# First two modulation vectors split between TensorE and VectorE, squares summed by TensorE, last value rows in groups of 256

## The chip, the cores and the metric

The kernel runs on one core of a Trainium2 chip. The metric is device time in microseconds (us), the median of several executions. One further execution is recorded by the hardware profiler; all rows below come from it. Engines: PE is TensorE (PEld its weight loads, which overlap its matmuls), DVE is VectorE, ACT is ScalarE, POOL is GpSimd, SP is SyncE, which here issues the loads of all weights. "L690" is line 690 of the kernel's file. The changed file has other line numbers.

## The reference, cut to what matters

Two layers over x of 256 rows and 2048 columns, all in fp32: the first mixes by RWKV-7, the second by banded attention, each with an MLP. Each layer takes six modulation vectors from c. The change touches the start of the first layer: the first two vectors (`sh1`, `sc1`), the norm, and the value product `xv @ w_v`.

```python
mod = c @ w_ada[layer] + b_ada[layer]
sh1, sc1, gt1, sh2, sc2, gt2 = jnp.split(mod, 6, axis=-1)
h = modulate(rms_norm(x, g_mix[layer]), sh1, sc1)     # h * (1 + scale) + shift

# rwkv7_time_mix
xx = token_shift(h) - h
xr, xw, xk, xv, xa, xg = [h + xx * mu[j] for j in range(6)]
r = xr @ w_r
k = xk @ w_k
v = xv @ w_v
w_log = -jax.nn.softplus(-(w0 + jnp.tanh(xw @ w1) @ w2)) - 0.5
a = jax.nn.sigmoid(a0 + (xa @ a1) @ a2)
g = jax.nn.sigmoid(xg @ g1) @ g2
...
```

## The kernel before

Activations lie transposed: the 2048 columns of x are 16 tiles n of 128 partitions, and the 256 rows of the sequence lie along the free dimension. Every weight comes from HBM once, in tiles of 512 KB (128 partitions by 1024 values). fp32 products are made of three passes: `halves` splits a weight tile `raw` into a rounded part wH (a cast on ACT, L378) and the rest wL (a subtraction on DVE, L381), `split` does the same for an activation (aHL), and PE adds wH by high, wH by low and wL by high. Products that PE does in plain fp32 stand as two records each in the profile.

The change lies in `layer_a`, in what runs before the key and receptance products, whose first matmul is L412 (tile pj). That stretch is a loop over the 16 tiles n. For each n it needs the modulation of these 128 columns, then it normalises and modulates h (L770 on DVE, L772 on ACT), takes the shift difference xx on POOL (L727), mixes it six times on DVE (L732 and L796), and PE multiplies: the first layers of the three small products (tile l, L779 and L783, plain fp32), and row block n of w_v for the first 1024 value columns (tile v, L787 to L789, weight rows `w_v_rows`), which adds up in PSUM over all n. The other 1024 value columns don't fit in PSUM. `v_part` does them for four n at once: each of its 16 tiles of w_v (4 groups of n by 4 blocks of 256 columns) gives one 512-wide sum in tile t (L751 to L753), which ACT copies (group 0) or DVE adds (L759) to the values in SBUF. From n = 4 on one `v_part` runs in each step; four are left at the end.

The first two modulation vectors are computed inside this loop, by `ada_blocks`, a generator that `next(adab)` drives a few tiles ahead of their use. A block is 256 columns of both vectors (`blocks` = eight times 2 column tiles). For each vector SP loads four tiles rawa (L673), each of 512 rows by 256 columns in pieces of 1 KB. Three of them go to PE: `crep` holds each value of c repeated over 32 columns, and four groups of 32 partitions of the PE array work on four row blocks at once (L690, tile m). The fourth goes to DVE, which multiplies by c and adds (L679 once, L682 three times, tile acca), and PE sums that over partitions (L684). ACT copies the block's result out (L697), PE turns it into columns and sums the four groups (L702), and DVE adds the bias and makes the gain (L708, L710). The tiles rawa have 6 buffers: the load of a tile waits until the tile six before it has been read.

The sum of squares of the norm: ACT squares (L514, L517), DVE adds (L518), PE sums over partitions with ones (L523), and `rstd` makes the reciprocal root.

The order of instructions on an engine isn't that of the code: the framework's scheduler interleaves it. SP's loads go out in its order, one behind the other; a load without a free buffer holds up all behind it. L368 is the load of all other weight tiles (raw), L763 that of the small products' weights. Later in the kernel the other ten vectors are computed on DVE alone (L452 and L454, tile acc, which has one buffer).

Of the kernel before, what the change touches and what calls it, by code (L numbers as in the profile page):

```python
# [18 lines left out]
P = 128  # L19
D = 2048  # L20
# [309 lines left out]
class Body:  # L330
# [242 lines left out]
    def run(self):  # L573
# [12 lines left out]
        for layer in (0, 1, "kv"):  # L586
            for part in range(2 if layer == "kv" else 6):
                self.mods[(layer, part)] = gp.tile([P, KT], F32, name=f"mod_{layer}_{part}")
        self.nhalf, self.pool_every = 0, 0
# [40 lines left out]
    def layer_a(self, st, sp):  # L630
# [6 lines left out]
        with ExitStack() as s1:  # L637
# [7 lines left out]
            first = CST_AT["ident"][0]  # L645
# [7 lines left out]
            crep = pb.tile([P, KT, 32], F32, name="crep")  # L653
            nc.vector.tensor_copy(crep, self.ct.unsqueeze(2).to_broadcast([P, KT, 32]))
            nc.vector.memset(h[:, :, 0:1], 0.0)
            gain = self.gp.tile([P, KT], F32, name="gain_g_mix0")

            blocks = [1] * 0 + [2] * ((KT - 0) // 2)

            def ada_blocks():  # L660
# [3 lines left out]
                for w_ in blocks:  # L664
                    W, ks = w_ * P, 8 // w_
                    ps = self.psm().rearrange("p (i n) -> p i n", i=2)
                    for part in (1, 0):
                        w, _ = self.ada_src(0, part)
                        w = w[:, lo * P:lo * P + W].rearrange("(a i p) n -> a p i n", p=P, i=ks)
                        for a in range(KT // ks):  # L670
                            raw = pb.tile([P, HK * P], F32, tag="rawa", bufs=6, name="rawa")
                            raw = raw.rearrange("p (i n) -> p i n", i=ks)
                            nc.sync.dma_start(out=raw, in_=w[a])  # L673
                            if a == KT // ks - 1:
                                acc = pb.tile([P, W], F32, tag="acca", bufs=2, name="acca")
                                for i in range(ks):
                                    ck = self.ct[:, ks * a + i:ks * a + i + 1]
                                    if i == 0:
                                        nc.vector.tensor_scalar(out=acc, in0=raw[:, i, :], scalar1=ck, scalar2=0.0,  # L679
                                                                op0=ALU.mult, op1=ALU.add)  # L680
                                    else:
                                        nc.vector.scalar_tensor_tensor(out=acc, in0=raw[:, i, :], scalar=ck, in1=acc,  # L682
                                                                       op0=ALU.mult, op1=ALU.add)
                                nc.tensor.matmul(ps[0:32, part, :W], self.cst("ones")[:, 0:32], acc,  # L684
                                                 start=False, stop=(part == 0), tile_position=(0, 0))
                            else:
                                for i in range(ks):
                                    kt = ks * a + i
                                    g = 32 * (kt % 4)
                                    nc.tensor.matmul(ps[g:g + 32, part, :W], crep[:, kt, :], raw[:, i, :],  # L690
                                                     start=(part == 1 and kt < 4),
                                                     stop=(part == 0 and g > 0 and kt >= KT - ks - 4),
                                                     tile_position=(0, g))
                            if part or a < KT // ks - 1:
                                yield
# [511 lines left out]
```

## Time and profile before

| | |
|---|---|
| median of 3 runs | 2673.8 us (2673.53 to 2674.96) |
| the profiled execution, its own time | 2673.81 us |
| its span | 2672.0 us |
| first L690, last L690 | 9.96 us, 172.37 us |
| first normalised row (L770) | 32.63 us |
| first L412 (pj) | 209.0 us |
| HBM read, mean over the span | 656.72 MB, 247 GB/s |

How to read the rows that follow. A row of windows has the stretch in us, its length, then for each engine its busy time and instructions, the TensorE clock that was granted (1.00 is full), the mean busy share of the 16 DMA engines (an estimate, which can come out a little over 1) and their rate. A row of the timeline has start, duration (of a row of several: from the first's start to the last's end), engine, line, operation, tile written and tiles read, count, and in brackets the engine's idle time ahead of it with what ended it. A row of groups has the count, then busy us and mean ns of one, then idle time. A matmul's duration contains its way through the array: matmuls in a row start every 0.12 us while each shows 0.28.

### The profile page before, as it was taken

How to read it: one execution, taken by the hardware profiler on the slowest of the kernel's cores; microseconds unless marked ns; L12 is line 12 of the kernel's file. 1: busy time of each engine (PE TensorE's matmuls, PEld its weight loads, DVE VectorE, ACT ScalarE, POOL GpSimd, SP SyncE). 2: the span in 40 equal slices, each digit the busy share in tenths (PEclk: the TensorE clock that was granted, in tenths of full speed). 3: DMA queues.
4: the chain of work that ended last, by engine and by line, in shares of the span. 5: the costliest groups of instructions: out<-in, count | busy, mean ns of one | idle time of the engine just before them, and what ended most of it. 6: DMA issues, size and time to landing. Idle time of an engine off the chain costs nothing. (4 is left out here: it accounts for less than half of the span.)

```text
span 2672.0 us, 58365 instructions
## 1 busy us (share of the span) xinstructions
PE 2600.1 (97%) x23690; PEld 2225.4 (83%) x23690; DVE 2101.0 (79%) x3109; ACT 1343.9 (50%) x2432; POOL 209.7 (8%) x320
## 2 busy tenths in 40 slices
PE   6999999999999999999999999999999999999997
PEld 3777788788899888888888998877898888888886
DVE  5778888889789888888888898899887556555555
ACT  3345555555456445355365554565564463453554
POOL 0001322332110000000000100000100000000002
PEclk9999999999999999999999999999999999999999
DMA  9966556565768888899898679887766555555553
GB/s 337 314 236 211 192 173 210 189 206 195 245 240 304 324 309 321 322 324 331 320 328 294 238 240 325 324 274 259 264 216 237 186 187 188 189 186 185 189 189 119
DMA packets 217390, 662.64 MB, mean 248 GB/s; under 512 B 21408, under 2 KB 68896, under 8 KB 217120
## 3 DMA queue, kind: packets, MB, share of 16 engines
q1 hardware_dynamic: 215056, 656.36, 71.1%
q8 instruction: 186, 3.05, 0.5%
q10 hardware_dynamic: 2064, 2.54, 0.3%
q14 instruction: 84, 0.69, 0.1%
HBM read 656.72 MB, written 2.10 MB: 247 GB/s over the span
## 5 line engine op out<-in xcount | busy, mean ns | idle before, releaser
L381 DVE TENSOR_TENSOR wL<-raw,wH 128x1024 fp32r<-128x1024 f32 x772 | 940.9, 1220 | 342.6 <-ACT wH L378 337.8
L378 ACT CAST wH<-raw 128x1024 fp32r<-128x1024 f32 x772 | 805.5, 1045 | 801.2 <-PE pj L412 646.0
L412 PE MATMUL pj<-aHL,wH 128*128 128x512 f32 x3328 | 1201.9, 403 | 2.0 <-DVE x L927 1.1
L413 PE MATMUL pj<-aHL,wL 128*128 128x256 f32 x3328 | 936.3, 281 | 0.0
L412 PEld LDWEIGHTS pj<-aHL,wH 128*128 128x128 f32 x3328 | 629.5, 189 | 154.1 <-issue 9.2
L412 PE MATMUL pj<-hHL,wH 128*128 128x512 f32 x2048 | 724.6, 399 | 0.0
L413 PEld LDWEIGHTS pj<-aHL,wL 128*128 128x128 f32 x3328 | 629.7, 189 | 2.6 <-issue 0.8
L413 PE MATMUL pj<-hHL,wL 128*128 128x256 f32 x2048 | 574.7, 281 | 0.0
L412 PEld LDWEIGHTS pj<-hHL,wH 128*128 128x128 f32 x2048 | 384.8, 188 | 95.7 <-DVE hHL L973 0.2
L413 PEld LDWEIGHTS pj<-hHL,wL 128*128 128x128 f32 x2048 | 387.0, 189 | 0.1
L454 DVE SCALAR_TENSOR_TENSOR acc<-rada,ct,acc 128x1024 f32<-128x1024 f32 x256 | 327.5, 1279 | 8.4 <-DMA rada<-w_ada 7.5
L518 POOL TENSOR_TENSOR ss<-ss,sq 128x256 f32<-128x256 f32 x56 | 54.5, 974 | 1590.8 <-ACT sq L517 1590.5
L998 DVE SCALAR_TENSOR_TENSOR x<-pj,mod,x 128x256 f32<-128x256 f32 x256 | 123.3, 482 | 59.5 <-PE pj L413 55.7
L454 DVE SCALAR_TENSOR_TENSOR acc<-raw,ct,acc 128x1024 f32<-128x1024 f32 x104 | 136.4, 1312 | 15.5 <-DMA raw<-w_ada 15.4
L401 PE MATMUL pj<-aHL,wH 128*128 128x258 f32 x384 | 109.0, 284 | 0.0
L402 PE MATMUL pj<-aHL,wH 128*128 128x258 f32 x384 | 109.0, 284 | 0.0
L970 ACT ACTIVATE t<-t 128x256 f32<-128x256 f32 x112 | 46.8, 418 | 122.6 <-DVE t L942 122.6
L403 PE MATMUL pj<-aHL,wL 128*128 128x258 f32 x384 | 108.0, 281 | 0.0
L403 PEld LDWEIGHTS pj<-aHL,wL 128*128 128x128 f32 x384 | 73.2, 191 | 0.2
L402 PEld LDWEIGHTS pj<-aHL,wH 128*128 128x128 f32 x384 | 72.6, 189 | 0.1
L401 PEld LDWEIGHTS pj<-aHL,wH 128*128 128x128 f32 x384 | 72.2, 188 | 0.2
L972 ACT ACTIVATE t<-t 128x256 f32<-128x256 f32 x128 | 53.4, 417 | 3.4
(244 smaller groups left out, 2812.3 us busy)
## 6 DMA issues: line engine op xcount, KB each, us to landing
raw<-w_up SPq DMA_DIRECT2D x256, 512.0 KB, 4.1
raw<-w_down SPq DMA_DIRECT2D x256, 512.0 KB, 4.1
rada<-w_ada SPq DMA_DIRECT2D x209, 512.0 KB, 5.7
raw<-w_ada SPq DMA_DIRECT2D x111, 512.0 KB, 4.4
rawa<-w_ada SPq DMA_DIRECT2D x64, 512.0 KB, 6.8
rada<-w_ada_kv SPq DMA_DIRECT2D x64, 512.0 KB, 6.6
raw<-w_k SPq DMA_DIRECT2D x32, 512.0 KB, 4.2
raw<-w_r SPq DMA_DIRECT2D x32, 512.0 KB, 4.5
```

What stands on the lines that cost most here:

```text
L378: nc.scalar.copy(Hf, raw)
L381: eng.tensor_tensor(out=Lf, in0=raw, in1=Hf, op=ALU.subtract)
L401: nc.tensor.matmul(ps, H[:, i, :], a(kt)[:, 0, :], start=(first and kt == 0), stop=False)
L402: nc.tensor.matmul(ps, H[:, i, :], a(kt)[:, 1, :], start=False, stop=False)
L403: ins = nc.tensor.matmul(ps, L[:, i, :], a(kt)[:, 0, :], start=False, stop=(last and kt == KT - 1))
L412: nc.tensor.matmul(ps, H[:, i, :], a(kt), start=(kt == 0), stop=False)
L413: ins = nc.tensor.matmul(ps[:, 0, :], L[:, i, :], a(kt)[:, 0, :], start=False, stop=(kt == KT - 1))
L454: nc.vector.scalar_tensor_tensor(out=self.acc, in0=raw, scalar=ck, in1=self.acc, op0=ALU.mult, op1=ALU.add)
L518: (eng or nc.gpsimd).tensor_tensor(out=self.ss, in0=self.ss, in1=sq, op=ALU.add)
L970: nc.scalar.activation(t, t, AF.Relu)
L972: nc.scalar.activation(t, t, AF.Square)
L998: nc.vector.scalar_tensor_tensor(out=x, in0=ps[:, i, :], scalar=self.mods[(layer, 5)][:, n:n + 1], in1=x, op0=ALU.mult, op1=ALU.add)
```

## The change

1. The vectors. For the first 1024 rows of w_ada, blocks of columns still go to PE (L690 in the new file too). For the other 1024 rows the host passes the weights transposed (`w_ada0_t`): a tile is 128 output columns on the partitions by 1024 rows along the free dimension, rows of 4 KB. DVE multiplies it by `crow`, those 1024 values of c on every partition, and sums along the free dimension in the same instruction (L696, `accum_out`). The result is already a column per output; DVE adds it to bias and PE's part (L711, L713). The L684 products are gone. `crow` is made at the start: DVE puts the values of c on diagonals of a 128 by 1024 tile (L665, in a buffer of rawa), PE sums it over partitions with ones (L670), ACT copies (L671). It lies in the buffer that L452 uses later.
2. The blocks are seven of 2 column tiles and two of 1. A block of 1 loads pieces of 512 bytes for PE.
3. The squares are summed by 16 matmuls with ones into one PSUM tile (L726), and the root is taken before the first block. The ones and the identity are in the first load of constants.
4. The value tiles of the last four n are cut into 2 n by 512 columns (`parts`): such a tile leaves two sums, in the PSUM tiles t and m. Four `v_part` go with the steps n = 14 and 15 (two each), two are left behind the loop.

```diff
-    def rstd(self):
+    def rstd(self, ps=None):
         nc = self.nc
-        ps = self.psm()[:, :T]
-        nc.tensor.matmul(ps, self.cst("ones"), self.ss, start=True, stop=True)
+        if ps is None:
+            ps = self.psm()[:, :T]
+            nc.tensor.matmul(ps, self.cst("ones"), self.ss, start=True, stop=True)
...
-            crep = pb.tile([P, KT, 32], F32, name="crep")
-            nc.vector.tensor_copy(crep, self.ct.unsqueeze(2).to_broadcast([P, KT, 32]))
+            crep = pb.tile([P, HK, 32], F32, name="crep")
+            nc.vector.tensor_copy(crep, self.ct[:, :HK].unsqueeze(2).to_broadcast([P, HK, 32]))
...
-            blocks = [1] * 0 + [2] * ((KT - 0) // 2)
+            sums = pb.tile([P, 2, KT], F32, name="sums01")
+            rawa = lambda: pb.tile([P, HK * P], F32, tag="rawa", bufs=6, name="rawa")
+
+            crow, diag = self.wp.tile([P, HK * P], F32, tag="acc", bufs=1, name="crow"), rawa()
+            nc.vector.tensor_tensor(out=diag.rearrange("p (k n) -> p k n", n=P),
+                                    in0=self.cst("ident").unsqueeze(1).to_broadcast([P, HK, P]),
+                                    in1=self.ct[:, HK:].unsqueeze(2).to_broadcast([P, HK, P]), op=ALU.mult)
+            for i in range(0, HK * P, 512):
+                ps = pp.tile([P, 512], F32, tag="t", bufs=1, name="t")
+                nc.tensor.matmul(ps, self.cst("ones"), diag[:, i:i + 512], start=True, stop=True)
+                nc.scalar.copy(crow[:, i:i + 512], ps)
+
+            blocks = [2] * 7 + [1] * 2
...
-                        for a in range(KT // ks):
-                            raw = pb.tile([P, HK * P], F32, tag="rawa", bufs=6, name="rawa")
-                            raw = raw.rearrange("p (i n) -> p i n", i=ks)
+                        for a in range(w_):
+                            raw = rawa().rearrange("p (i n) -> p i n", i=ks)
                             nc.sync.dma_start(out=raw, in_=w[a])
...
+                            raw = rawa()
+                            nc.sync.dma_start(out=raw, in_=d["w_ada0_t"][KT * part + lo + a])
+                            nc.vector.scalar_tensor_tensor(out=raw, in0=raw, scalar=1.0, in1=crow, op0=ALU.mult,
+                                                           op1=ALU.mult, accum_out=sums[:, part, lo + a:lo + a + 1])
...
-            self.ss_reset()
+            ss = pp.tile([P, 2, T], F32, tag="v3", bufs=1, name="v3")[:, 0, :]
             for n in range(KT):
-                self.ss_add(h[:, n, 1:T + 1], n, nc.vector)
+                sq = pb.tile([P, T], F32, tag="sq", bufs=3, name="sq")
+                nc.scalar.activation(sq, h[:, n, 1:T + 1], AF.Square)
+                nc.tensor.matmul(ss, self.cst("ones"), sq, start=(n == 0), stop=(n == KT - 1))
+            r = self.rstd(ss)
...
+            parts = [(4 * g, 4, i) for g in range(3) for i in range(4)]
+            parts[11:] = [(12, 2, 0), parts[11], (12, 2, 1), (14, 2, 0), (14, 2, 1)]
...
-                if n >= 4:
-                    v_part(n // 4 - 1, n % 4)
+                for _ in range((n >= 4) + (n >= KT - 2)):
+                    v_part()
...
-            for i in range(4):
-                v_part(3, i, "tm"[i % 2])
+            for _ in range(2):
+                v_part()
```

What the scheduler makes of it, at three places. SP's first loads (h is x, lw1 the small products' weights), before:

```order
L648 DMA h_100<-x 128x4x256 x2
L673 DMA rawa_161<-w_ada 128x4x256
L673 DMA rawa_167<-w_ada 128x4x256
L673 DMA rawa_173<-w_ada 128x4x256
L673 DMA rawa_179<-w_ada 128x4x256
L673 DMA rawa_187<-w_ada 128x4x256
```

and now:

```order
L652 DMA h_99<-x 128x4x256 x2
L781 DMA lw1_247<-lora1 128x448
L368 DMA raw_249<-w_v_rows 128x1024
L686 DMA rawa_181<-w_ada0 128x4x256
L695 DMA rawa_187<-w_ada0_t 128x1024
L686 DMA rawa_190<-w_ada0 128x4x256
L695 DMA rawa_196<-w_ada0_t 128x1024
L686 DMA rawa_199<-w_ada0 128x4x256
L695 DMA rawa_205<-w_ada0_t 128x1024
L686 DMA rawa_208<-w_ada0 128x4x256
L695 DMA rawa_214<-w_ada0_t 128x1024
L686 DMA rawa_252<-w_ada0 128x4x256
```

The small products' weights and the first value rows (which stood behind the eighth tile) have moved ahead of the first; tiles for PE and for DVE alternate. With the diagonal in the first buffer, rawa_208 takes the buffer of rawa_181.

PE at the start, before (ss is the sum of squares):

```order
L690 MATMUL m<-rawa,crep 32x256 x12
L684 MATMUL m<-acca,csts 32x256
L690 MATMUL m<-rawa,crep 32x256 x12
L684 MATMUL m<-acca,csts 32x256
L702 MATMUL m<-csts,adat 32x1 x16
L523 MATMUL m<-ss,csts 128x256
```

and now (v_122 is the sum of squares, t the copy of c):

```order
L670 MATMUL t<-rawa,csts 128x512
L726 MATMUL v_122<-sq,csts 128x256
L670 MATMUL t<-rawa,csts 128x512
L726 MATMUL v_122<-sq,csts 128x256 x3
L690 MATMUL m<-rawa,crep 32x256
L726 MATMUL v_122<-sq,csts 128x256 x12
L690 MATMUL m<-rawa,crep 32x256 x15
L706 MATMUL m<-csts,adat 32x1 x16
```

All but one of the L690 of the first block stand behind the sixteen L726 now, where the one product with ones stood behind the whole block.

PE around the last tile of the modulation, before:

```order
L690 MATMUL m_1630<-rawa_1756,crep_109 32x256 x4
L789 MATMUL v1_249<-aHL_246,wL_1801 128x256
L789 MATMUL v2_250<-aHL_246,wL_1801 128x256
L787 MATMUL v2_250<-aHL_246,wH_1800 128x256
L788 MATMUL v2_250<-aHL_246,wH_1800 128x256
L789 MATMUL v2_250<-aHL_246,wL_1801 128x256
```

and now:

```order
L690 MATMUL m_1568<-rawa_1669,crep_108 32x128 x8
L807 MATMUL v1_242<-aHL_239,wL_1705 128x256
L807 MATMUL v2_243<-aHL_239,wL_1705 128x256
L805 MATMUL v2_243<-aHL_239,wH_1704 128x256
L806 MATMUL v2_243<-aHL_239,wH_1704 128x256
L807 MATMUL v2_243<-aHL_239,wL_1705 128x256
L807 MATMUL v3_244<-aHL_239,wL_1705 128x256
L706 MATMUL m_1684<-csts_65,adat_1682 32x1 x8
```

Both stand in the middle of the products of n = 13. From that L690 to the first pj there are 234 rows before and 222 now. The last L706 follows seven rows behind its L690, where the last L702 stood 34 rows behind; the last L684, between them, is gone. From the first pj on, the order on PE is the same row for row, and so are SP's loads from the first of w_k on.

More of the change, by code (lines that the diff above doesn't have):

```diff
@@ L664, in ada_blocks @@
                 for w_ in blocks:
[L665 removed]
+                    W, ks = w_ * P, HK // w_
                     ps = self.psm().rearrange("p (i n) -> p i n", i=2)
                     for part in (1, 0):
[L668 to L694 removed]
```

78 lines of the change are left out of this document (52 added, 26 removed).

## The prediction

> **What bounds the kernel now.** The page comes first, for the whole; the question is which stretch can give or lose time.
>
> ```profile
> span 2672.0 us, 58365 instructions
> PE 2600.1 (97%) x23690; PEld 2225.4 (83%) x23690; DVE 2101.0 (79%) x3109; ACT 1343.9 (50%) x2432; POOL 209.7 (8%) x320
> ```
>
> PE is busy for 97% of the span, so time comes only from PE's own work or from stretches where it waits. The change lies ahead of the key and receptance products, whose first matmul (L412) starts at 209.0 us. The windows of that stretch, cut where its loop over n repeats (two values of n are one block of modulation columns):
>
> ```profile
> core 0: us, PE busy (x) PEld busy (x) DVE busy (x) ACT busy (x) POOL busy (x), PEclk, DMA share, GB/s
> 2.00:64.00 62.00, 38.81 (x338) 23.76 (x339) 39.72 (x91) 18.35 (x38) 2.55 (x4) 0.92 1.04 348
> 64.00:86.00 22.00, 20.91 (x194) 15.58 (x193) 15.46 (x33) 7.38 (x12) 1.90 (x2) 1.00 0.96 324
> 86.00:108.00 22.00, 21.54 (x198) 16.12 (x198) 15.54 (x33) 7.88 (x13) 1.85 (x2) 1.00 0.92 312
> 108.00:130.00 22.00, 21.62 (x200) 16.29 (x199) 16.15 (x34) 7.38 (x12) 1.85 (x2) 1.00 0.92 306
> 130.00:152.00 22.00, 20.54 (x192) 15.48 (x191) 16.41 (x35) 7.10 (x11) 1.53 (x2) 1.00 0.92 308
> 152.00:174.00 22.00, 20.98 (x195) 15.83 (x194) 16.43 (x35) 7.11 (x11) 1.54 (x2) 1.00 0.92 314
> 174.00:208.00 34.00, 32.18 (x269) 29.52 (x267) 22.04 (x36) 19.07 (x26) 1.53 (x2) 1.00 0.41 139
> ```
>
> Three parts. Up to 64 us the transfers run at 348 GB/s with nothing to spare, and PE is busy for only 38.81 of 62 us. From 64 to 174 us there are five equal cycles of 22 us: PE 21.1 us busy on average (96%), the transfers at 0.92 to 0.96, 6.9 MB a cycle. From 174 us PE works off what is left, with the transfers at 0.41. Who holds the transfers back in the middle part is in the waits of SP's queue:
>
> ```profile
> SPq L673 <- PE m L690: 54.0, 22, 4.9
> ```
>
> Tile loads wait for a buffer that PE's L690 has yet to read, 54.0 us in 110. Part of that is the ordinary wait of a queue that runs ahead, but the share falls from 1.04 to 0.92 just where PE's busy share rises to 96%, so I read the cycles as set by PE, with the transfers close behind.
>
> **The change, cycle by cycle (64 to 174 us).** What the first two vectors cost in the first and last cycle: first all that reads the raw tiles, then the L684 alone:
>
> ```profile
> 64.00:86.00 22.00, 4.23 (x48) 1.16 (x48) 3.53 (x8) 1.00 0.96 324
> 152.00:174.00 22.00, 4.23 (x48) 1.16 (x48) 3.60 (x8) 1.00 0.92 314
> 64.00:86.00 22.00, 1.24 (x4) 0.28 (x4) 1.00 0.96 324
> ```
>
> *PE.* Six tiles a cycle cost 4.23 us (0.705 each), the two sums over partitions 1.24. Now four tiles are left and L684 is gone: 2 x 0.705 + 1.24 = 2.65 us less, 21.1 becomes 18.5.
>
> *VectorE.* It spent 3.56 us a cycle on two tiles and now takes four, each in one instruction that multiplies 1024 columns and sums them. No row has that sum; the nearest is L454, of the same operation, shape and type without it:
>
> ```profile
> L454 DVE SCALAR_TENSOR_TENSOR acc<-rada,ct,acc 128x1024 f32<-128x1024 f32 x256 | 327.5, 1279 | 8.4 <-DMA rada<-w_ada 7.5
> L682 DVE SCALAR_TENSOR_TENSOR acca<-rawa,ct,acca 128x256 f32<-128x256 f32 x30 | 14.4, 479 | 0.5
> 400.00:500.00 100.00, 98.78 (x2037) 80.97 (x2032) 88.06 (x163) 54.29 (x154) 28.45 (x39) 1.00 0.64 211
> ```
>
> From below 1.28 us; from above a second pass over the columns: (1279 - 479) / 768 = 1.04 ns a column, so 1.07 us more, 2.35. I take 1.28, as L454 already reads two fp32 tensors. Four make 5.1: VectorE goes from 16.0 to 17.6 us a cycle. The two or three tiny instructions on 2 to 4 columns stay about as they were.
>
> The Trainium skill, Vector Engine (DVE) Microarchitecture Reference, section 7 (Points that are easy to get wrong), speaks against this: a scalar-tensor-tensor with two SBUF sources that are not bf16 halves its throughput, with no port left for the accumulator. L454 at 1.25 ns a column shows no halving for two sources alone; with an accumulator nothing here shows it. By the rule the instruction would cost the upper end, which is the second rival.
>
> *Transfers.* The bytes are the same, 64 tiles of 512 KB, but half come as rows of 4 KB in place of 1 KB. The price of a packet from two stretches of the DMA view, 2 to 64 us and 1100 to 1500 us (packets, MB, share of the 16 engines' time):
>
> ```profile
> q1 hardware_dynamic: 17058, 19.67, 95.0%
> q1 hardware_dynamic: 34257, 124.73, 86.7%
> ```
>
> 62 x 16 x 0.95 / 17058 = 55 ns for 1153 bytes, 400 x 16 x 0.867 / 34257 = 162 ns for 3641: 0.043 ns a byte and 6 ns a packet. A tile takes 1.59 us in 1 KB rows, 1.45 in 4 KB, 1.77 in 512-byte rows. A transposed tile saves 0.14 us, 0.55 a cycle; the four 512-byte tiles of the last two blocks, now one column tile wide, cost 0.7 together. A cycle's 6.9 MB at the 350 GB/s that the first part holds are 19.7 us, less 0.55: 19.15.
>
> So PE 18.5, VectorE 17.6, transfers 19.15: the transfers set the cycle. At the 96% that PE reaches now that is 20.0 us. Five cycles gain 2.0 each, less 0.7: **-9.3 us**. Bounds: -14 (five times 19.15, no loss) and 0 (the three disturb each other as much as now).
>
> **The start.** The squares are now added by 16 fp32 matmuls of 256 columns, ahead of most L690 in PE's order, with two of 512 columns that copy c along the partitions. SP loads the first value rows ahead of the first tile, and one of the six buffers first holds the diagonal.
>
> ```profile
> 9.96 1.08 PE L690 MATMUL m<-rawa,crep 128*32 128x256 f32 x8 [9.96 <-DMA rawa<-w_ada]
> 10.41 0.42 ACT L514 ACTIVATE ss<-h 128x256 f32<-128x256 f32 x1 [8.39 <-DMA h<-x]
> 32.63 0.88 DVE L770 SCALAR_TENSOR_TENSOR h<-h,gain_g_mix,rstd 128x256 f32<-128x256 f32 x2
> 39.58 1.56 PE L783 MATMUL l<-mix,lw 128*128 128x256 f32 x4
> 41.20 0.28 PE L787 MATMUL v<-aHL,wH 128*128 128x256 f32 x1
> 41.32 0.28 PE L788 MATMUL v<-aHL,wH 128*128 128x256 f32 x1
> 145.50 1.02 PE L779 MATMUL l<-mix,lw 128*96 128x256 f32 x4
> 146.36 1.03 PE L783 MATMUL l<-mix,lw 128*128 128x256 f32 x4
> 1.00:21.00 20.00, 3.48 (x28) 0.84 (x32) 5.81 (x15) 5.80 (x13) 0.00 (x0) 1.00 1.01 327
> ```
>
> Such a matmul (two records) takes 0.78 us early (L783 at 39.58) and 0.43 once PE runs steadily (145.50 to 146.36). Sixteen, and four more for the two wide ones, are 8.6 to 15.6 us from the first square at 10.8: done at 19.4 to 26.4. I take 22.5: PE begins without a pause, but from idle. Until then the fourth tile for PE has no buffer, and SP stands at it with all behind: the second block's tiles, the next value rows. What is issued before are about 6.8 MB (x, constants, value rows, lora, six tiles), which at 327 GB/s last until 22 us. With some 2.5 us from the release to the data, the transfers pause for 3 us (bounds 0 and 7). Against that 14 transposed tiles before 64 us save 2.0: **+1.0 us**. The first normalised row may come earlier than 32.63 us; behind transfers that are full this is worth nothing, and its cover, if it goes, is worth up to 3 us of gain. The removed 16 adds on VectorE hid behind the loads.
>
> **The tail.** From the last tile's matmuls at 172.37 us to 209.0 PE does 36.6 us.
>
> ```profile
> 172.37 0.64 PE L690 MATMUL m<-rawa,crep 128*32 128x256 f32 x8
> ...
> 174.36 0.28 PE L753 MATMUL t<-aHL,wL 128*128 128x256 f32 x1
> 174.48 0.28 PE L751 MATMUL t<-aHL,wH 128*128 128x256 f32 x1
> ...
> 175.91 0.28 PE L751 MATMUL t<-aHL,wH 128*128 128x256 f32 x1
> 176.11 0.62 PE L684 MATMUL m<-acca,csts 128*32 128x256 f32 x2
> 176.66 0.38 PE L752 MATMUL t<-aHL,wH 128*128 128x256 f32 x1
> L412 PE MATMUL pj<-aHL,wH x93: 388/397/697, 209.0 to 259.6; 128*128 128x512 f32 x93
> ```
>
> The order has 234 rows there before and 222 now: 12 x 0.12 = 1.4 us less; L684 (0.75 against 0.12) saves 0.6. The last value products leave two 512-column sums each, four adds more; VectorE has room (22.04 of 34 us), and PE fills the other bank meanwhile, so I cost them at nothing; without that cover about 0.7 us each. **-2.0 us**, bounds -2.3 and +0.8. The number of products is the same; that they come in an earlier order is what makes the 12 rows.
>
> **The sum.** -9.3 + 1.0 - 2.0 = -10.3 us. From the first pj on PE's order is the same, and PE is the bound (98.78 of 100 us in the row above), so the shift is carried whole. The profiled execution took 2673.81 us, 1.8 more than its span, and the median shown is 2673.8: 2663.5 us.
>
> **The rivals.**
>
> *The buffers keep the cycle (2669).* PE was not what held the transfers: tiles come in turns from two engines, SP issues in order, and a tile that waits in VectorE's queue behind weight halves stops everything behind it. For it: the 0.92 in cycles where PE still pauses for about 1 us. Against it: L690 as the named releaser. The cycle falls only to 21.2, five times -0.8, with start and tail -5.
>
> *VectorE becomes the bound (2686).* The accumulating instruction takes 2.35 us: 16.0 - 3.56 + 9.4 = 21.8 us a cycle. VectorE never did more than 88 of 100 us beside PE (the row of 400 to 500 us), so the cycle is 24.8, +2.8 five times, with start and tail +13. It decides from about 1.74 us an instruction on: (22 x 0.88 - 12.4) / 4. Against it: L454.
>
> *The start stalls (2672).* PE stays slow through all the sums, the transfers pause 7 us and the cycles gain only 1 each: +5 - 5 - 2.
>
> *More than the sum (2657).* The early first row lets PE run ahead, and the cycles reach 19.15.
>
> **How the numbers follow.** Chances: forecast 0.53, buffers 0.2, VectorE 0.1, start 0.07, more 0.1. 0.2% is 5.3 us, what a measurement here can tell from nothing. Faster by that, below 2668.5: nearly all of the forecast, the last rival and four tenths of the buffers: 0.70. Within: 0.21. Slower: 0.09. The range runs from the last rival's 2656 to 2675, where a mild case of VectorE ends.
>
> **What will show it.** Right: L696 at 1.3 us; cycles of about 20 us with the transfers at 0.95 or more; the last L690 near 163 us and the first pj matmul near 199. Wrong: L696 above 1.7 us; a gap in the transfers of over 5 us near 22 us; cycles still at 22 us; or the time lost again behind the first pj matmul.

## The result and the profile after

| | before | after |
|---|---|---|
| median | 2674.1 us (2670.4 to 2678.0, 20 runs) | 2669.1 us (2664.5 to 2675.5, 20 runs) |
| ratio, 95% interval | | 0.9983 (0.9977 to 0.9989) |
| span of the profiled execution | 2672.0 us | 2667.0 us |
| last L690, first pj (L412) | 172.4, 209.0 us | 169.3, 203.1 us |

The change gains 5.0 us, half of the 10.3 forecast. It is faster by 0.17% (the interval lies below 1), inside the range, and it lands on the price of a rival (2669).

The windows of the changed kernel, cut at the same times as those of the kernel before:

```profile
2.00:64.00 62.00, 45.99 (x358) 31.47 (x358) 39.87 (x82) 20.89 (x44) 4.30 (x5) 0.92 1.01 358
64.00:86.00 22.00, 19.96 (x170) 15.31 (x171) 16.70 (x34) 6.58 (x11) 1.64 (x2) 0.92 0.87 304
86.00:108.00 22.00, 19.59 (x180) 15.64 (x179) 17.45 (x34) 7.96 (x13) 1.19 (x2) 1.00 0.89 311
108.00:130.00 22.00, 19.79 (x181) 15.85 (x179) 17.41 (x34) 8.78 (x14) 1.80 (x3) 1.00 0.95 322
130.00:152.00 22.00, 19.25 (x176) 15.60 (x176) 18.59 (x37) 7.06 (x12) 1.53 (x2) 1.00 0.94 308
152.00:174.00 22.00, 20.69 (x213) 17.54 (x214) 20.33 (x45) 7.26 (x14) 2.70 (x2) 1.00 0.84 294
```

In the four windows from 64 to 152 us PE's busy time fell from 21.1 to between 19.3 and 20.0 us, and VectorE's rose from about 16 to between 16.7 and 18.6. But the transfers do not run faster: 304 to 322 GB/s, as before (306 to 324). So PE was relieved and the cycles did not follow. The groups that read rawa in the changed kernel (count, ns min/median/max, first and last start):

```profile
L690 PE MATMUL m<-rawa,crep x288: 272/379/637, 17.8 to 169.3; 128*32 128x256 f32 x112, 128*32 128x128 f32 x32
L696 DVE SCALAR_TENSOR_TENSOR rawa<-rawa,crow x32: 1209/1218/1428, 17.5 to 171.1; 128x1024 f32<-128x1024 f32 x32
L696 DVE DVE_READ_ACCUMULATOR rawa<-rawa,crow x32: 72/82/85, 18.7 to 172.2; 128x1 f32 x32
```

To see where the 5.9 us at the first pj come from, a mark for each cycle is needed. SP issues one lw load for each n; the 6th, 8th, 10th, 12th and 14th stand one block apart:

| kernel | 6th lw | 8th | 10th | 12th | 14th | mean cycle | last L690 | first pj |
|---|---|---|---|---|---|---|---|---|
| before | 63.8 | 85.5 | 107.5 | 129.5 | 152.2 | 22.1 | 172.4 | 209.0 |
| after | 61.9 | 84.4 | 106.2 | 127.4 | 149.0 | 21.8 | 169.3 | 203.1 |

The start gains 1.9 us (63.8 to 61.9), the four cycles 1.3 together, the stretch with the last block nothing, and the tail, from the last L690 to the first pj, 2.7 (36.6 to 33.9). Behind the first pj 0.9 are lost again: the spans differ by 5.0.

These marks are of one execution each. How far they can be trusted is shown by pairs of kernels of the section on the experiments that have the same order of instructions on every engine up to 150 us: the changed kernel and e3, and e2 and e5. Their marks differ by up to 1.9 us, and the four cycles together take 87.1 us in the changed kernel and 88.6 in e3 (88.4 before). So the 1.3 us of the cycles is not clear of chance. That the 14th lw comes 3 us earlier or more is: 152.2 before (154.0 in e4), 147.7 to 149.2 in the changed kernel, e1, e2, e3 and e5.

What a cycle looks like from SP and PE, in the timeline of the changed kernel (rows of other engines left out):

```profile
52.34 0.38 SPq L686 DMA_DIRECT2D rawa<-w_ada  x1
...
61.68 0.43 PE L706 MATMUL m<-csts,adat 128*32 128x1 f32 x32
...
62.87 0.50 SPq L695 DMA_DIRECT2D rawa<-w_ada_t  x1
...
64.65 0.39 PE L769 MATMUL t<-aHL,wL 128*128 128x256 f32 x1 [1.60 <-DVE wL L381]
...
66.37 2.02 PE L797 MATMUL l<-mix,lw 128*96 128x256 f32 x4 [0.63 <-DVE mix L739]
68.33 1.08 PE L690 MATMUL m<-rawa,crep 128*32 128x256 f32 x8
69.47 0.38 SPq L686 DMA_DIRECT2D rawa<-w_ada  x1
```

SP issues nothing from 62.87 to 69.47 us. It waits for the buffer of the tile that it issued at 52.34 (six loads back). That load landed after 8.5 us, so the tile lay in its buffer from 60.8 on; PE read it at 68.33, because in PE's order its L690 stand behind value products (L767 to L769) and the row's L797, and those wait for VectorE.

A second stop, 76.43 to 81.94, ends with a tile of VectorE's. The tile was issued at 62.87 and landed after 8.1 us, at 71.0, but in VectorE's order its L696 stands behind two subtractions of weight halves (L381), and these wait for value rows that SP could only issue at 71.88, after the first stop:

```profile
71.88 0.53 SPq L368 DMA_DIRECT2D raw<-w_v_rows  x1
...
78.40 2.36 DVE L381 TENSOR_TENSOR wL<-raw,wH 128x1024 fp32r<-128x1024 f32 x2 [3.19 <-DMA raw<-w_v_rows]
80.68 1.22 DVE L696 SCALAR_TENSOR_TENSOR rawa<-rawa,crow 128x1024 f32<-128x1024 f32 x1
81.94 0.33 SPq L695 DMA_DIRECT2D rawa<-w_ada_t  x1
```

So the stops feed each other: a late reader holds up the queue, the loads behind it go out late, and the engines that wait for those are the next late readers. The profile's chain of work that ended last runs through this load too, from 60 to 110 us:

```profile
71.88 6.53 DMA raw<-w_v_rows
```

I read the circle from this one cycle; no run cuts it at one place only. Over the four cycles (64 to 152 us) SP's waits for these buffers are shared about equally between the two engines:

```profile
SPq L686 <- PE m L690: 26.9, 10, 6.0
SPq L695 <- DVE rawa L696: 25.2, 9, 5.6
```

What the two stops do to the transfers, in windows of the same kernel:

```profile
64.00:68.00 4.00, 2.72 (x11) 1.84 (x11) 3.49 (x6) 1.35 (x3) 1.64 (x2) 0.79 1.06 397
68.00:72.00 4.00, 4.00 (x26) 2.76 (x26) 4.00 (x11) 0.81 (x2) 0.00 (x0) 0.78 0.61 192
78.00:82.00 4.00, 3.24 (x24) 2.74 (x23) 3.60 (x5) 1.31 (x2) 0.00 (x0) 1.00 1.00 360
82.00:88.00 6.00, 5.33 (x74) 4.41 (x73) 3.55 (x8) 2.76 (x5) 0.10 (x1) 1.00 0.72 221
```

Between the stops the transfers run at 360 to 397 GB/s, behind each they drop to some 200. A cycle's mean of 310 hides both.

### The profile page after: what moved, and what is told of

Its sections match the earlier page's. It is cut to its first block, busy times and chain, and to the rows that moved or that the text cites. A ratio compares the mean times of both kernels' runs of the same rounds, so it can differ in the third digit from the quotient of the medians.

```text
span 2667.0 us, 58173 instructions
## 1 busy us (share of the span) xinstructions
PE 2594.2 (97%) x23596; PEld 2229.2 (84%) x23596; DVE 2112.8 (79%) x3102; ACT 1345.2 (50%) x2435; POOL 208.7 (8%) x320
## 4 chain that ended last, share of the span: by engine, by line
PE 85%; DVE 5%; issue 4%; DMA 4%; ACT 2%; POOL 1%; DVEq 0%; SPq 0%; ACTq 0%; POOLq 0%
PE pj L412 45%; PE pj L413 23%; PE pj L402 2%; PE pj L401 2%; PE pj L403 2%; DMA raw<-w_ada 1%; DVE wL L381 1%; PE iv L111 1%; DVE acc L454 1%; PE gr L105 1%; ACT wH L378 1%; PE ms L115 1%; PE o L401 1%; PE ms L324 0%; PE ms L105 0%
## 5 line engine op out<-in xcount | busy, mean ns | idle before, releaser
L381 DVE TENSOR_TENSOR wL<-raw,wH 128x1024 fp32r<-128x1024 f32 x772 | 941.1, 1220 | 354.9 <-ACT wH L378 347.0
L412 PE MATMUL pj<-aHL,wH 128*128 128x512 f32 x3328 | 1202.0, 403 | 1.9 <-DVE x L945 1.4
L412 PEld LDWEIGHTS pj<-aHL,wH 128*128 128x128 f32 x3328 | 629.4, 189 | 154.4 <-issue 8.7
L412 PE MATMUL pj<-hHL,wH 128*128 128x512 f32 x2048 | 723.0, 398 | 0.0
L412 PEld LDWEIGHTS pj<-hHL,wH 128*128 128x128 f32 x2048 | 384.6, 188 | 94.4 <-DVE hHL L991 0.2
L454 DVE SCALAR_TENSOR_TENSOR acc<-rada,ct,acc 128x1024 f32<-128x1024 f32 x256 | 327.2, 1278 | 8.5 <-DMA rada<-w_ada 7.6
L454 DVE SCALAR_TENSOR_TENSOR acc<-raw,ct,acc 128x1024 f32<-128x1024 f32 x104 | 136.2, 1309 | 15.3 <-DMA raw<-w_ada 14.9
```

Source lines behind the costliest of these rows:

```text
L381: eng.tensor_tensor(out=Lf, in0=raw, in1=Hf, op=ALU.subtract)
L412: nc.tensor.matmul(ps, H[:, i, :], a(kt), start=(kt == 0), stop=False)
L454: nc.vector.scalar_tensor_tensor(out=self.acc, in0=raw, scalar=ck, in1=self.acc, op0=ALU.mult, op1=ALU.add)
```

## The experiments

"The changed kernel" is the base where nothing else is said. All were timed beside the kernel before on the same chip; ratios are to that, with 95% intervals.

**e1, a seventh buffer for rawa** (room from one `sq` buffer less).

```diff
-            rawa = lambda: pb.tile([P, HK * P], F32, tag="rawa", bufs=6, name="rawa")
+            rawa = lambda: pb.tile([P, HK * P], F32, tag="rawa", bufs=7, name="rawa")
```

> The changed kernel with 7 buffers for the raw modulation tiles in place of 6 (and 2 for the squares in place of 3). Theory A: in the cycles from 64 us on no L690 waits for data, so TensorE and VectorE, held to each other by their fixed orders, set the cycle of 21.5 us, and the transfers only wait for them: one more buffer changes the first pj matmul (203.1 us) by less than 1 us and the total by less than 2 us. Theory B: the buffers set the cycle, tiles for two engines come in turns and a late one stops the queue: a seventh buffer takes the cycle to about 20.5 us, five cycles gain 4 to 5 us, first pj near 198.5 us, total near 2664 where before is 2674.

Measured: 2669.6 us, ratio 0.9983 (0.9974 to 0.9991). Mean cycle 21.6, last L690 170.4. One more buffer alone is worth nothing that shows.

**e2, squares on VectorE again**, root behind the first block.

```diff
-                nc.tensor.matmul(ss, self.cst("ones"), sq, start=(n == 0), stop=(n == KT - 1))
-            r = self.rstd(ss)
+                self.ss_add(h[:, n, 1:T + 1], n, nc.vector)
```

> The changed kernel with the squares added by VectorE and the root behind the first block again. Theory A: the start is full of transfers either way (0 to 64 us), so the place of the sum is worth little: first pj within 1.5 us of 203.1, total within 2 us of the changed kernel (2669). Rival: the early root lets the first rows start at 28.5 us in place of 32.6 and this lead is what is left at the end: first pj and total 3 to 4 us later, near 2672.5.

Measured: 2668.2, 0.9976 (0.9968 to 0.9985). The first normalised row comes at 32.3 us in place of 28.5, and the 10th lw is at 106.1 as in the changed kernel. The squares on PE bring the first row forward and gain nothing.

**e3, the old cut of the last value rows.**

```diff
-            parts = [(4 * g, 4, i) for g in range(3) for i in range(4)]
-            parts[11:] = [(12, 2, 0), parts[11], (12, 2, 1), (14, 2, 0), (14, 2, 1)]
+            parts = [(4 * g, 4, i) for g in range(4) for i in range(4)]
```

> The changed kernel with the last value tiles cut as before (4 n by 256 columns, four value products behind the loop). If the tail of 33.9 us (36.6 before) owes its 2.7 us to the gone L684 and the shorter wait for the last block, the first pj stays within 1 us of 203.1 and the total within 1.5 us of 2669. Rival: the new cut fills TensorE's waits near the end, and undoing it costs 3 us or more: near 2672.

Measured: 2666.9, 0.9977 (0.9967 to 0.9987). Last L690 at 169.3 as in the changed kernel, but the first pj at 201.1, 2.0 us earlier. Neither expectation had that: undoing the cut gains. PE's waits from 168 to 204 us in the changed kernel and from 168 to 202 in e3:

```profile
PE t L767 <- DVE v L777: 2.5, 2, 2.1
```

```profile
PE t L768 <- DVE wL L381: 0.8, 1, 0.8
```

With the new cut PE waits 2.1 us at one place for VectorE to add up the sums and so free their PSUM tile; with the old cut that wait is not there.

**e4, the new cut alone in the kernel before** (part 4 of the change, nothing else).

> The kernel before with only the new cut of the last value tiles. The order has as many rows behind the last L690 as before, so I expect no change beyond 1 us in the first pj (209.0) and in the total (2674). Rival: the cut alone gives 3 us or more, near 2671.

Measured: 2676.0, 1.0008 (1.0000 to 1.0017); last L690 174.8, first pj 212.4, a tail of 37.6 against 36.6. The first pj comes 3.4 us later where at most 1 was expected; 1.8 of this stand already at the 14th lw, up to which the order is that of the kernel before. PE's waits from 174 to 213 us show the same cause:

```profile
PE t L760 <- DVE v L770: 3.0, 3, 2.0
PE pj L412 <- DVE v L770: 0.9, 1, 0.9
```

**e5, the split alone**: e2 and e3 together.

> The changed kernel with both of its side edits undone: the squares are added by VectorE and the root is taken behind the first block as before, and the last value rows are cut as before; only the split of the first two vectors is left. What the runs so far say (squares alone undone 2668.2, cut alone undone 2666.9, changed kernel 2669.1 to 2669.6): if the side edits are worth nothing, 2666 to 2668, ratio about 0.997, last L690-type matmul at 169 as in the others. Rival, the side edits carry part of the gain only together: 2670 or more.

Measured: 2665.6, 0.9965 (0.9953 to 0.9978): as expected. Tail 31.8 us (167.5 to 199.3). The split alone carries the gain. That the new cut gives a part of it back is in the traces: the tail is 33.8 to 35.0 us with it (the changed kernel, e1, e2) and 31.8 without (e3, e5). The times only lean that way, since the interval of e5 touches that of the changed kernel.

**e6, VectorE relieved.** Three quarters of each sum are left out.

```diff
-nc.vector.scalar_tensor_tensor(out=raw, in0=raw, scalar=1.0, in1=crow, op0=ALU.mult,
+nc.vector.scalar_tensor_tensor(out=raw[:, :256], in0=raw[:, :256], scalar=1.0, in1=crow[:, :256], op0=ALU.mult,
```

> VectorE relieved: the sum over a transposed tile takes 256 of its 1024 columns (three quarters of that sum are left out), 0.91 us less for each, 3.7 us of VectorE in a cycle of four; loads, buffers and TensorE as in the changed kernel, where a cycle takes 21.2 to 22.5 us. Theory, TensorE and VectorE hold each other at the block's end and the transfers only follow: cycles of 20.0 to 20.8 us, last L690 near 163, time near 2662. Rival, the transfers or TensorE alone set the cycle: 21.2 to 21.8 us as now, last L690 at 168 to 170, 2667 to 2670.

Measured: 2671.3, 0.9987 (0.9978 to 0.9996). Mean cycle 21.65 against 21.8, last L690 169.0: next to nothing, with 3.7 us of VectorE's work gone. My theory of that time (TensorE and VectorE hold each other through the amount of their work) expected 20.0 to 20.8 and missed. A part of what VectorE saved it spent waiting for PE at the end of each block (64 to 152 us, the changed kernel, then e6):

```profile
DVE mods L713 <- PE m L706: 5.5, 4, 1.5
```

```profile
DVE mods L713 <- PE m L706: 12.3, 4, 3.1
```

The place of the sums in VectorE's order stayed what it was: in e6 too SP stands from 96.13 to 100.84 us for an L696 behind two L381 that began at 98.10. So e6 speaks against the amount of VectorE's work as what sets the cycle, though the scheduler moved other instructions on PE and VectorE too; it says nothing against a tile that waits in VectorE's order. The first pj came at 201.3, yet the span is 2670.3: some 5 us were lost behind it, which I can't explain.

**e7, TensorE relieved.** One of three products of the last value tiles is left out.

```diff
-                        nc.tensor.matmul(ps, H[:, j, :], b, start=False, stop=False)
```

> TensorE relieved: of the three products of the last value tiles the middle one is left out (16 matmuls of 0.29 us in a cycle, 4.6 us of TensorE's 19.8); VectorE, loads and buffers as in the changed kernel. Theory, TensorE and VectorE hold each other: TensorE's part of the chain is shorter, cycles 20 to 21 us, no less, since VectorE's 18 us and its waits stay. Rival, TensorE alone sets the cycle: down to 18 to 19 us, where VectorE's 18 and the transfers' 19 end it; last L690 at 157 to 160. Rival, the transfers set it: 21.2 to 21.8 us as now.

Measured: 2670.1, 0.9981 (0.9972 to 0.9991). The cycles grew, to 22.8 us, and the last L690 came at 174.8. No theory had that. Two windows of e7:

```profile
86.00:90.00 4.00, 3.13 (x11) 2.52 (x11) 3.49 (x5) 1.87 (x4) 1.75 (x2) 0.57 0.97 372
90.00:94.00 4.00, 4.00 (x20) 2.43 (x20) 4.00 (x10) 0.73 (x2) 0.00 (x0) 0.58 0.29 76
```

PE got just over half of its clock for 8 us, and in the second half of that the transfers stood almost still (76 GB/s). Over the four cycles the mean granted clock was 0.90, against 0.98 in the changed kernel. The instruction order moved too, so what the clock alone cost is not shown, and neither is what less work on PE does at the same clock: e7 doesn't decide whether PE's work sets the cycle.

**e8, the loads relieved.** Half of each transposed tile is loaded and read twice, into a tile of its own; the other half of that sum is left out. The engines do the same amount of work. Room for that tile comes from one `sq` buffer less.

```diff
-nc.sync.dma_start(out=raw, in_=d["w_ada0_t"][KT * part + lo + a])
-nc.vector.scalar_tensor_tensor(out=raw, in0=raw, scalar=1.0, in1=crow, op0=ALU.mult,
+nc.sync.dma_start(out=raw[:, :512], in_=d["w_ada0_t"][KT * part + lo + a][:, :512])
+nc.vector.scalar_tensor_tensor(out=junk.rearrange("p (i n) -> p i n", i=2), in0=raw[:, :512].unsqueeze(1).to_broadcast([P, 2, 512]), scalar=1.0, in1=crow.rearrange("p (i n) -> p i n", i=2), op0=ALU.mult,
```

> Transfers relieved: of each transposed tile only 512 columns are loaded and the sum reads them twice into a tile of its own (the other half of that sum is left out); VectorE and TensorE do as much as before. A cycle then moves 5.7 MB in place of 6.75. Theory, the transfers only follow the engines: cycles of 21.2 to 21.8 us as now, the transfer engines' share down to 0.78. Rival, the transfers set the cycle: 18.3 us by the bytes, ended by TensorE's 19.8: about 20 us, last L690 near 161, time near 2661.

Measured: 2653.8, 0.9925 (0.9911 to 0.9939). Mean cycle 19.2, last L690 150.4, first pj 188.9. The time fell further than even the rival of the expectation, that the loads set the cycle, had said. The stretch from 64 to 152 us in e8, then in the changed kernel:

```profile
64.00:152.00 88.00, 85.72 (x861) 71.13 (x862) 82.19 (x161) 35.68 (x57) 11.64 (x9) 1.00 0.89 303
64.00:152.00 88.00, 78.59 (x702) 62.40 (x702) 70.14 (x136) 30.36 (x49) 6.16 (x9) 0.98 0.91 311
```

Now PE is busy for 85.7 of 88 us, 18.7 in a cycle of 19.2: here PE is the bound. In the changed kernel it is busy for 78.6 of 88, so there it is not.

But the bytes are not all that changed. SP's loads go out in the same order as in the changed kernel; the instructions on PE and VectorE do not. In the changed kernel VectorE waits for PE at the end of each block (the L713 above, 5.5 us in four cycles), and the next row hangs on that. In e8 L713 stands between the mixes of the row before, and VectorE waits for it nowhere from 64 to 152 us:

```profile
77.09 0.48 DVE L739 SCALAR_TENSOR_TENSOR mix<-xx,vecs,h 128x256 f32<-128x256 f32 x1
77.49 0.15 DVE L713 TENSOR_TENSOR mods<-sums,m 128x4 f32<-128x4 f32 x1
77.56 0.48 DVE L739 SCALAR_TENSOR_TENSOR mix<-xx,vecs,h 128x256 f32<-128x256 f32 x1
```

So e8 shows what fewer bytes and this other order do together. Which of the two took the cycle to 19.2 is open; a run with the bytes of one and the order of the other would decide, and there is none.

**e9, earlier reading of the tiles.** The loads' rate has the stops in it, so the next question was whether the place of L690 in PE's order makes them. Two steps of the next block (a tile for PE, one for VectorE) are written a row earlier; nothing is added or left out. The order on SP, PE and VectorE moves with it.

```diff
-                ahead = 5 if n + 2 < KT and ends[n + 1] == n + 2 else 0
+                ahead = 0 if n + 2 >= KT else 6 if ends[n + 1] == n + 2 else 2
```

> The changed kernel with two steps of the next block (one tile for TensorE, one for VectorE) written one row earlier, and six in place of five at the row after, so that in TensorE's order the next block's first L690 stand right behind the L706 of the block before instead of behind nine or more value matmuls and the row's L797. Nothing is left out or added. Theory, a cycle is the transfers' 19 us at their full rate plus the stretch in which SP waits for a buffer whose tile landed long before (62.87 to 69.47 and 76.43 to 81.94 us in the changed kernel) because its L690 stand late in TensorE's order: that stretch shrinks, cycles of 19.5 to 20.8 us in place of 21.8, last L690 at 162 to 166, time 2661 to 2666. Rival, the rate of the transfers alone sets the cycle, or what is moved ahead on TensorE only moves the wait to the row behind it: 21.4 to 22 us as now, last L690 at 168 to 170, 2667 to 2670.

Measured: 2665.6, 0.9962 (0.9949 to 0.9976), below the changed kernel's interval (0.9977 to 0.9989), if barely. Last L690 166.0, first pj 200.3. PE's order around one block's end in e9:

```profile
82.13 0.43 PE L706 MATMUL m<-csts,adat 128*32 128x1 f32 x32
...
84.37 0.64 PE L690 MATMUL m<-rawa,crep 128*32 128x256 f32 x8
...
87.61 1.10 PE L797 MATMUL l<-mix,lw 128*96 128x256 f32 x4 [0.51 <-DVE mix L739]
```

L690 now stands 2.2 us behind L706 and ahead of L797, where it stood 6.7 us behind it. The two cycles from the 8th to the 12th lw (83.5, 103.6, 123.8) take 20.1 and 20.2 us, at 327 and 336 GB/s where the changed kernel has 311 and 322:

```profile
86.00:108.00 22.00, 20.46 (x186) 16.39 (x184) 18.45 (x37) 8.25 (x15) 1.18 (x2) 1.00 0.93 327
108.00:130.00 22.00, 20.09 (x180) 16.15 (x180) 19.33 (x37) 9.31 (x14) 1.18 (x2) 1.00 0.96 336
```

The cycles ahead of and behind these two take 22.7 and 23.6, so the mean stays at 21.6 and the expectation is half met: of the 2.8 us gained at the first pj 1.0 are there at the 6th lw, 0.6 come in the four cycles and the rest behind them. Two stops a cycle remain (75.20 to 81.36 and 86.85 to 92.06). What SP waits for has changed, not how long (64 to 152 us, to compare with the two rows of the changed kernel):

```profile
SPq L686 <- PE m L690: 45.5, 14, 6.8
SPq L695 <- DVE rawa L696: 7.5, 6, 2.0
```

The tiles of VectorE are now mostly read in time, and the queue waits for those of PE instead.

**e10, the same in the split alone.**

> The same earlier steps in the kernel with the split alone (squares on VectorE, old cut of the last value rows; 2665.6 without the earlier steps). Theory, the wait for a buffer behind TensorE's order is part of every cycle: 2658 to 2662. Rival: 2664 to 2667 as without.

Measured: 2663.1, 0.9958 (0.9945 to 0.9970), 1 us above the theory's range and 1 below the rival's. Mean cycle 20.9 against 21.55 in e5, last L690 165.9 against 167.5, first pj 198.4 against 199.3. It is the fastest kernel that computes all, below both kernels; against e5 the intervals overlap.

**e11, blocks of two throughout** in e10.

```diff
-            blocks = [2] * 7 + [1] * 2
+            blocks = [2] * 8
```

> The best version so far (split alone, two steps earlier, 2663.1) with eight blocks of two rows in place of seven and two of one. The last two blocks of one row load rows of 512 bytes, and SP stands still from 155.50 to 164.15 us there. If the narrow blocks cost what they load in small pieces, about 2 us less: 2660 to 2662. If they earn more by ending the last block's chain early (first pj behind a block of one row and not of two), 2664 to 2667.

Measured: 2667.2, 0.9973 (0.9963 to 0.9982). The trace has the last L690 at 162.2 and the first pj at 196.3, 2.1 us before e10's. But the 57th tile load, the first that the edit changes, goes out at 131.80 in e11 and at 133.36 in e10: 1.6 us of the lead are there before the edit acts and are chance. The time isn't better, and the profiled execution took 2465.9 us from the first pj to the end, 2463.3 in e10. Undecided.

**e12, the earlier steps in the kernel before.** The same line as in e9.

> The kernel before with the same two steps of the next block written one row earlier and nothing else. Theory, the wait for a buffer behind TensorE's order is a part of the cycle that the change neither made nor removed: the kernel before gains by the earlier steps too, 2669 to 2672, cycles of 20.5 to 21.7 us in place of 22.1. Rival, the wait is a product of the change's own order: 2673 to 2676 as the kernel before.

Measured: 2677.6, 1.0011 (1.0002 to 1.0020). The theory's 2669 to 2672 is refuted: there the earlier reading gains nothing. The profiled execution took 8.8 ms, so its trace says nothing of the cycles.

The marks of the runs, beside the table above (for e12 there are none):

| kernel | 6th lw | 8th | 10th | 12th | 14th | mean cycle | last L690 | first pj |
|---|---|---|---|---|---|---|---|---|
| e1 seventh buffer | 62.6 | 84.6 | 105.7 | 126.9 | 148.9 | 21.6 | 170.4 | 204.2 |
| e2 squares on VectorE | 62.7 | 84.3 | 106.1 | 127.3 | 149.2 | 21.6 | 169.3 | 204.3 |
| e3 old cut | 60.4 | 82.7 | 106.1 | 127.3 | 149.0 | 22.15 | 169.3 | 201.1 |
| e4 new cut in the kernel before | 64.7 | 86.4 | 108.4 | 130.4 | 154.0 | 22.3 | 174.8 | 212.4 |
| e5 split alone | 61.4 | 82.4 | 104.3 | 125.5 | 147.7 | 21.55 | 167.5 | 199.3 |
| e6 VectorE relieved | 59.9 | 82.3 | 104.1 | 125.0 | 146.5 | 21.65 | 169.0 | 201.3 |
| e7 TensorE relieved | 61.4 | 83.3 | 106.1 | 129.3 | 152.7 | 22.8 | 174.8 | 203.8 |
| e8 loads relieved | 56.3 | 76.6 | 95.3 | 114.0 | 132.9 | 19.2 | 150.4 | 188.9 |
| e9 earlier steps | 60.9 | 83.5 | 103.6 | 123.8 | 147.4 | 21.6 | 166.0 | 200.3 |
| e10 e5 with earlier steps | 61.2 | 82.8 | 103.7 | 123.8 | 144.8 | 20.9 | 165.9 | 198.4 |
| e11 e10 with blocks of two | 61.2 | 81.2 | 102.2 | 122.2 | 143.2 | 20.5 | 162.2 | 196.3 |

## Why the prediction was half right

**The time: inside the range, by other parts than forecast.** Of the 5.9 us at the first pj 4.6 come from the start and the tail, which were forecast to give 1.0 together, and 1.3 from the cycles, forecast to give 9.3. The direction was forecast; that the time still lies inside the range, with the main term nearly gone, is luck.

**L696: right.** 1.218 us, with 0.082 for a read of the accumulator as an instruction of its own: 1.30 against 1.28 expected. The second rival, VectorE as the bound, is gone with it. The rule of the Trainium skill (Vector Engine (DVE) Microarchitecture Reference, section 7, Points that are easy to get wrong), that a scalar-tensor-tensor with two non-bf16 SBUF sources halves its throughput, was priced as a second halving on top of L454, and that does not show: with the accumulator the instruction takes 1.19 ns a column, L454 without one 1.25. But the prediction also read L454 as "no halving for two sources alone", and that is wrong if the rule is meant against one source. Instructions with a single tensor source, in the kernel before:

```profile
L452 DVE TENSOR_SCALAR acc<-rada,ct x17: 741/745/746, 822.3 to 1986.0; 128x1024 f32<-128x1024 f32 x17
L679 DVE TENSOR_SCALAR acca<-rawa,ct x16: 335/346/353, 18.2 to 170.4; 128x256 f32<-128x256 f32 x16
```

That is (745 - 346) / 768 = 0.52 ns for each further column, half of the 1.04 that the prediction worked out for two sources.

**The engines' sums: near.** PE 18.5 us a cycle was forecast; the changed kernel has 78.6 of 88 us, 19.5 in a cycle of 21.8 (at a mean clock of 0.98), and e8, where PE is the bound, 18.7. VectorE 17.6; the four windows from 64 to 152 us give 70.2 of 88, 17.4 in a cycle of 21.8.

**The cycles: the step that failed.** -9.3 us was the sum's largest part; four cycles gave -1.3, and that is not clear of chance. The prediction took the largest of three sums, "the transfers set the cycle", and then "at the 96% that PE reaches now that is 20.0 us". The 96% was PE's share in the kernel before, and the transfers were given it without a row that shows it. With 19.15 us of transfers in a cycle of 21.8 they reach 88%. What takes the rest is in the timeline: SP's queue stops twice a cycle for 5 to 7 us, waiting for a buffer whose tile has landed but has not been read, about as often because of PE's order as because of VectorE's.

That the place of the reading makes a part of this is likely from e9, e10 and e11, where it was moved forward: single cycles of 19.9 to 20.2 us where the changed kernel, e1, e2, e3 and e5 have none below 21.0, and mean cycles of 21.6, 20.9 and 20.5 against 21.55 to 22.15. By the medians the time fell by 3.5 us (e9) and 2.4 (e10), but the intervals of e9 and the changed kernel barely part and those of e10 and e5 overlap. It is a part only: the stops do not vanish. That the bytes set the cycle beside them isn't shown, since e8 changed the order too. Why a seventh buffer gives nothing isn't settled either.

Also, the 350 GB/s behind the 19.15 was itself a mean over the start; between stops the transfers reach 360 to 397.

**The rival "The buffers keep the cycle" (2669, chance 0.2)** had the time right and the mechanism nearer than the forecast: SP in order, and a tile that waits in an engine's order. It laid this on VectorE's queue behind weight halves, and the second stop above is just that; the first is PE's, and over the four cycles the two weigh about the same (25.2 and 26.9 us). Its sum was not right in its parts: it had the cycles at 21.2 (21.8 measured) and the start and tail at -1 (-4.6), so its time is in part luck too.

**What set the cycle before.** I read it as PE, at 96%. The runs agree but don't prove it: earlier reading, by the medians worth 3.5 us in the changed kernel, gains nothing before (e12), as one would expect if PE has no time to spare there. PE relieved, or the loads, in the kernel before would decide; that wasn't tried.

**The start: +1.0 forecast, -1.9 measured.** The squares end at 24.1 us (22.5 was taken), and the pause is there. Windows of the changed kernel, then of e2, where VectorE adds the squares:

```profile
20.00:30.00 10.00, 7.46 (x90) 4.74 (x88) 6.54 (x16) 5.50 (x13) 0.40 (x1) 0.94 0.82 279
30.00:64.00 34.00, 28.80 (x250) 21.67 (x250) 29.35 (x62) 10.10 (x19) 3.90 (x5) 0.87 1.06 382
```

```profile
20.00:30.00 10.00, 4.09 (x54) 1.53 (x58) 8.01 (x21) 3.83 (x10) 0.00 (x0) 1.00 1.06 376
30.00:64.00 34.00, 30.01 (x258) 21.65 (x258) 30.18 (x66) 10.60 (x21) 3.83 (x4) 1.00 0.96 337
```

From 20 to 30 us the changed kernel moves 0.97 MB less than e2, 2.6 us at e2's rate: near the 3 us of the forecast. But e3, with the same order up to there, has 340 GB/s in that window, so a part of the pause is of this one execution. Then the changed kernel and e3 both run at 382 GB/s up to 64 us and e2 at 337, so the loss is made up. The step that failed was to take the transfers for full there ("348 GB/s with nothing to spare"): they had spare. What lets them use it isn't shown. The early first row does not explain the gain, since e5, where it comes at 31.8 us, has its 6th lw at 61.4, no later than the changed kernel.

**The tail: -2.0 forecast, -2.7 measured, for another reason.** The split alone is worth -4.8 (36.6 to 31.8 in e5), and the new cut takes 2.1 back. From the last L690 to the first pj, before, in the changed kernel and in e5:

```profile
172.40:209.00 36.60, 33.92 (x284) 30.73 (x284) 23.72 (x38) 20.01 (x27) 1.53 (x2) 1.00 0.43 146
169.30:203.10 33.80, 30.93 (x259) 28.95 (x251) 26.25 (x43) 19.53 (x27) 1.12 (x2) 1.00 0.47 160
167.50:199.30 31.80, 30.62 (x258) 29.00 (x248) 23.68 (x38) 19.42 (x26) 1.04 (x2) 1.00 0.51 165
```

PE's own work fell by 3.0 to 3.3 us, where 2.0 had been counted; its pauses fell from 2.7 to 1.2 in e5 but are 2.9 with the new cut. "I cost them at nothing" is the step that failed: the adds have no cover at one place, where PE stands 2.1 us for a PSUM tile. The bound of 0.7 for each of four adds was right in kind.

**Carried whole behind the first pj: nearly.** 5.9 us there, 5.0 at the end. The difference is within what one execution differs from another: from the first pj to the end, with the same instructions on PE and VectorE (on PE all but some 60 of 22120 in the same order), the traces take 2461.5 us (e4) to 2469.0 (e6).

## What to carry to other kernels

A stage that is fed by one in-order queue through a ring of buffers can be slower than the largest of its sums: look in the timeline for the stretches in which the queue issues nothing, take the load six (or however many buffers) back, and compare when it landed with when it was read. A queue's sum of waits says little here, since it stays the same (57.5 us from 64 to 152 in the changed kernel, 58.3 in e9 for the three largest entries); the rate in short windows and the engines that it waits for say more. An edit that relieves one engine or the loads also makes the scheduler move instructions: compare the orders before putting the effect down to the relief. And measure side edits one by one: here one of three carried the gain, and one cost 2 us of it in the traces.

## What the hardware showed unexpectedly

PE's granted clock dropped here after quite short pauses. Windows of 2 us in the changed kernel:

```profile
62.00:64.00 2.00, 1.05 (x20) 0.62 (x8) 1.74 (x5) 1.39 (x4) 0.25 (x1) 1.00 1.00 355
64.00:66.00 2.00, 1.09 (x7) 0.88 (x7) 1.49 (x3) 0.99 (x3) 1.64 (x2) 1.00 1.09 397
66.00:68.00 2.00, 1.63 (x4) 0.96 (x4) 2.00 (x4) 0.36 (x1) 0.00 (x0) 0.58 1.02 398
68.00:70.00 2.00, 2.00 (x13) 0.87 (x13) 2.00 (x4) 0.41 (x1) 0.00 (x0) 0.57 0.59 238
```

PE is busy for 2.14 of 4 us, with no gap over 1.60 us, and then gets 0.57 of its clock for 4 us; the eight L690 of that moment take 1.08 us in place of the usual 0.64. The Trainium skill (TensorE: Matmul & The Clock Gate, Part 1) puts the abstract rule as no idle gaps of more than about 3.4 us. Here the clock dropped without such a gap. That it is the sum of the shorter pauses that counts is my reading; no run varies them alone.
